# Products of a conditioning vector with its weights, taken four units of weights at a time

## The chip, the core and the metric

The kernel runs on one core of a Trainium2 chip. The metric is the device time of one execution in microseconds (us); the time of a version is the median of its runs. In the profile PE is TensorE's products, PEld its loads of weights, DVE VectorE, ACT ScalarE, POOL GpSimd, SP the queue of SyncE, which here issues most transfers.

## The reference

Two blocks follow each other. The first has two layers over 512 latent tokens and, in its first layer, 256 context tokens, all of 1024 features, in fp32:

```python
def mixer_layer(x, cx, c, c_ctx, w_in, w_out, w_ada, b_ada, ...):
    shift, scale, gate = jnp.split(jax.nn.silu(c) @ w_ada + b_ada, 3, axis=-1)
    shift_c, scale_c, gate_c = jnp.split(jax.nn.silu(c_ctx) @ w_ada + b_ada, 3, axis=-1)
    h = x * (1.0 + scale[:, None]) + shift[:, None]
    hc = cx * (1.0 + scale_c) + shift_c
    (a_q, a_i, a_ff, a_fb, b_q, ...) = jnp.split(h @ w_in, SPLIT_AT, axis=-1)
    ...
    y = jnp.concatenate([y_a, y_b, y_c, y_d], axis=-1) * jax.nn.silu(g_lat)
    x_new = layer_norm(alpha * x + gate[:, None] * (y @ w_out), ln_g, ln_b)
```

The two conditioning vectors c and c_ctx have 1024 numbers each; w_ada has 1024 rows and 3072 columns in each layer. Mixer A (y_a) is a gated recurrence, B, C and D are attention of three kinds. Shift and scale of a layer are wanted before its h, the gate at the layer's end. The second block (a gated mixture of four branches and an MLP) doesn't use w_ada.

## The kernel before

**Products.** The large products (of h with w_in, for instance) are made from a high and a low part of either factor, in three products (`mm3`): each unit of weights, 128 x 1024 numbers, is loaded by SP's queue as `raw` and split into `whi` and `wlo` on whichever of ScalarE, VectorE and GpSimd is free. The products with w_ada are fp32 throughout and take `raw` as it is, 4,096 bytes in each partition. The stationary factor is `cs`, 128 rows by 32 columns, of which two hold silu(c) and silu(c_ctx) for one k (128 of the 1024 rows of w_ada). Four k's stand side by side in the array: k goes to column group q = k % 4 and to the PSUM rows 32q to 32q + 31, and k + 4 is added to the same rows. One fp32 product is two instructions in the profile. A chunk of 512 columns is 8 products (16 instructions) from 4 units with 2 k's each; a chunk of 256 columns is 8 products from 2 units with 4 k's each. A chunk's bank is then copied to SBUF by ScalarE (`row`), and a product with a matrix that selects adds the four groups (`co_mod` for shift and scale, the rest of `g_ada_gate` for the gate).

**Chunks.** Layer 0's shift and scale are made at the start in eight chunks of 256 columns. Layer 1's shift and scale are a filler named mod in layer 0: four chunks of 512 columns. Each layer's gate is a filler named gate: two chunks of 512 columns. So there are eight chunks of 512 columns.

**The order of the work.** The program is emitted by a planner that keeps estimates of when engines and data will be ready. Work in flight (attention in the order c, b, d of its mixers, with a few units at a time; the two pairs of mixer A; evacuations) is a list of generators that yield what they wait for. In each turn the first of them that is ready goes on; only when none is ready does the current filler go on (`turn`). Fillers are the products with w_in and w_ada. `choose` takes up the next one:

```python
early = f.name[1:2].isdigit() and any(x.name[:1] in "bd" for x in self.todo[:i])
if early and self.early >= self.cfg["early"][self.l] and not self.forced:
    continue
if f.need == 0 or self.M.live * Mem.G + f.need <= self.cfg["cap"] or self.forced:
```

`M.live * Mem.G` is the planner's account of SBUF in bytes of a partition, `cap` is 200,000. The written order of layer 0 behind c and v is `b fq0 d g4 g2 mod fq1 g0 gate g6 g5 g3 g7 g1`, that of layer 1 `b fq0 fq1 g4 g5 gate d mod g0 g2 g3 g1 g6 g7` (mod is left out there). b and d make keys, queries and values of two attention mixers (their needs are 28,000), fq0 and fq1 the q and the forget gates of mixer A's two pairs (25,000), g0 to g7 gate columns (12,000). `early` bars the g's while b or d is still to be taken. A pair of mixer A begins when its fq is through and the pair before it has ended; attention of d begins when b's units are through and d's keys are prepared.

The loader (`wfill`, called by `wnext` for each unit and by some fillers in between) keeps up to 2 units ready and 2 more loading. When one unit is ready it makes no second one if the account and 8,192 would pass `capw`, 194,000; a further raw unit wants 4,096 below it. When the current filler has no more units to load it calls `choose` for the next, and when no filler is left every turn does.

**The account in layer 0.** The unchanged program's own account reads, in bytes: 179,328 when mod is taken (behind fq0, past d and the g's); at the loader's next call 176,320 with one unit of mod, so 172,224 without; 186,048 when mod's first chunk begins; between 162,304 and 178,816 without the units of w_ada while the six chunks are emitted; 178,816 when gate is taken, 174,656 when fq1 is, 144,448 when d is. In layer 1 it reads 149,824 when gate is taken and 164,672 when d is, in gate's second chunk.

After the planner, the tile framework orders each engine's instructions once more; two neighbours in the code may be parted there. SBUF addresses follow from the recorded lifetimes of all pieces, and a piece that takes the place of an earlier one waits for its last reader.

Of the kernel before, what the change touches and what calls it, by code (L numbers as in the profile page):

```python
# [24 lines left out]
# column starts in w_in of the first block  # L25
# [5 lines left out]
# units of packed w_in  # L31
U_F, U_Q, U_G, U_C0, U_C1, U_C2, U_C3 = 0, 4, 6, 14, 18, 22, 26

# columns of the per-partition vectors
# [16 lines left out]
# broadcast rows  # L51
# [37 lines left out]
def pack(inp):  # L89
# [67 lines left out]
    # constants of the shapes  # L157
# [14 lines left out]
    # second block  # L172
# [32 lines left out]
class Quiet:  # L205
    """Stands for an engine while lifetimes are recorded."""
# [5 lines left out]
class Est:  # L212
    """Estimates, while instructions are emitted, of when engines and data will be ready: the order of emission follows."""
# [7 lines left out]
    def touch(self, ap):  # L221
        """The times of a tensor and the granules of it (128 elements) that ap covers."""
        key = (ap.tensor.name, ap.offset, ap.ap)
        hit = self.memo.get(key)
        if hit is None:
            row = ap.ap[0][0]
            at = np.zeros(1, np.int64)
            if len(ap.ap) > 1 and row > 128:
                at[0] = ap.offset % row
                for s, n in ap.ap[1:]:  # L230
                    if s and n > 1:
                        k = np.append(np.arange(0, n, max(1, 128 // abs(s))), n - 1)
                        at = np.unique((at[:, None] + s * k).ravel())
            at = np.unique(at // 128)
            hit = self.memo[key] = (key[0], at, int(at[-1]) + 1)
        name, at, need = hit
        for d in (self.w, self.r):
            if name not in d:
                d[name] = np.zeros(max(need, 48))
            elif len(d[name]) < need:  # L240
                d[name] = np.append(d[name], np.zeros(need - len(d[name])))
        return self.w[name], self.r[name], at
# [24 lines left out]
class Eng:  # L267
    """An engine whose instructions are timed as they are emitted."""
# [29 lines left out]
class Filler:  # L298
    """A stretch of the tensor engine's main work: its units of weights, and the memory it wants. A gate is taken up only
    after all before it."""  # L300
# [5 lines left out]
class Act:  # L306
    """Work in flight: a generator that yields what it waits for."""
# [6 lines left out]
class Tl:  # L314
    """A piece of SBUF with its own tensor."""
# [14 lines left out]
class Mem:  # L330
    """SBUF by lifetimes. A first emission (plan None) only records them; place() then gives each piece its address."""
# [29 lines left out]
    def place(self):  # L361
        """Addresses for the recorded lifetimes. After its last use a piece rests for as long as there is room elsewhere;
        the long-lived and then the larger pieces choose first."""
        n = len(self.log)
        size = np.array([r[0] for r in self.log])
        f0 = np.array([n + 1 if r[1] is None else r[1] for r in self.log])
        ends = [[] for _ in range(n + 2)]
        for i in range(n):
            ends[f0[i]].append(i)
        for share in np.arange(1.0, 0.5, -0.02):  # L370
            rest = f0.copy()
            resting, use = [], 0
            for t in range(n):
                resting += ends[t]
                use += size[t]
                while use > share * self.n and resting:
                    i = resting.pop(0)
                    rest[i] = t
                    use -= size[i]
            for i in resting:  # L380
                rest[i] = n + 1
            for long in (300, 100, 200, 500, 50):
                at = self.fit(size, f0, rest, long)
                if at is not None:
                    self.share = share, long
                    return at
        raise MemoryError(f"peak {self.peak * self.G} of {self.n * self.G}")
# [26 lines left out]
class Pb:  # L414
    """Banks of PSUM."""
# [9 lines left out]
class Psum:  # L425
# [3 lines left out]
    def pick(self, n, est):  # L429
        """The free banks that have been read first, and when."""  # L430
# [28 lines left out]
class K:  # L459
# [18 lines left out]
    # ---- short forms  # L478
# [3 lines left out]
    def best(self, n, **costs):  # L482
        """The engine that would be through first; costs in ns for each of n columns."""
# [43 lines left out]
    def scale(self, out, a, s):  # L527
        """out = a times a column s."""
# [21 lines left out]
    # ---- time  # L550
# [43 lines left out]
    # ---- work in flight  # L594
# [11 lines left out]
    def after(self, *keys):  # L606
        """Until no work of these keys is in flight."""
# [8 lines left out]
    def room(self, n):  # L616
        """Until n bytes more would fit; given up when nothing else can go on."""
# [60 lines left out]
    def choose(self):  # L678
        """Takes up the first filler for which there is room."""
# [20 lines left out]
    def filled(self, *names):  # L700
        """Until these fillers are through."""
        return self.until(lambda: all(n in self.ndone for n in names))

    def units(self, us, f, window):
        """f(u) for every u, up to so many at a time."""
# [11 lines left out]
    # ---- weights  # L717
# [28 lines left out]
    def more(self):  # L746
        """Weights of a further filler."""
# [17 lines left out]
    def g_fm(self, parts, evac):  # L765
        """parts: [(hi, lo, n)]; evac(i, bank) for each."""
# [15 lines left out]
    def g_tm(self, tiles, evac, pre=True, ku=2, rounds=None, hook=None):  # L782
        """tiles: [(t, hi(k) ap, lo(k) ap, columns)]; a unit of weights has ku k's; rounds: which units are gone through at
        a time."""
# [33 lines left out]
    # ---------------------------------------------------------------- setup  # L818
# [25 lines left out]
    def load_late(self):  # L844
        """Constants that are wanted later."""
# [22 lines left out]
    # ---------------------------------------------------------------- ada  # L868
# [11 lines left out]
    def g_ada_chunk(self, res, n=512):  # L880
        """The product with n columns, the k's in four parts of the rows."""
        yield (self.bank(),)
        ps = self.new_bank()
        for u in range(n // 128):
            raw, = self.wnext()
            yield (raw,)
            for kk in range(1024 // n):
                k = u * (1024 // n) + kk
                q = k % 4
                self.nc.tensor.matmul(ps[32 * q:32 * q + 32, :n], self.cs[:, k, :], raw[:, kk * n:(kk + 1) * n],  # L890
                                      start=k < 4, stop=k >= 4, tile_position=(0, 32 * q))
            self.M.free(raw)
# [20 lines left out]
    def g_ada_mod(self, l, js):  # L913
        """shift and 1 + scale, feature-major: mod[:, kind * 8 + k, (lat, ctx)]."""
# [57 lines left out]
    # ---------------------------------------------------------------- a layer  # L972
# [8 lines left out]
    def htiles(self, ncol):  # L981
        """ncol(t): columns for token tile t, 0 to leave it out."""
# [7 lines left out]
    def consts_layer(self, l):  # L990
# [14 lines left out]
        if l == 1:  # L1005
# [9 lines left out]
            # f = lb + (1 - lb) (1 + tanh) / 2  # L1015
# [5 lines left out]
    # fillers  # L1021
# [9 lines left out]
    def rope_tm(self, out, src, t, G, d, isq=False, e2="*"):  # L1031
        """out = rotated src, both [128, G, d]; queries come out times d^-0.5."""
# [12 lines left out]
    def g_c(self):  # L1045
        """Rotated k and q of mixer C, token-major."""
# [19 lines left out]
    def g_bd(self, which):  # L1066
        """k, q and v of mixers B and D: raw for B, rotated for D."""
# [33 lines left out]
    def g_fq(self, pair):  # L1101
        """2 silu(q) of two heads and their forget gates."""
# [24 lines left out]
    def g_g(self, m):  # L1127
        """2 silu of the gate columns of y[m]."""
# [9 lines left out]
    def yput(self, m, t):  # L1138
        """One of the two factors of 2 y[m]; the second one closes it."""
# [19 lines left out]
    # attention  # L1159
    def stack4(self, stage, dst, eng="*", n=4):  # L1160
        """Transposes n x [128, 128] of stage into dst [128, n, 128]."""
# [6 lines left out]
    def kstack(self, src, tag):  # L1168
        """src(t) gives a staged [128, 512] for each key tile."""
# [10 lines left out]
    def stage_c(self, raw, p, t, isq):  # L1180
        """[128, 4, 32]: keys hi hi lo lo, queries hi lo hi lo."""
# [9 lines left out]
    def stage_k64(self, src):  # L1191
        """[128, 2, 64] keys: hi hi, lo lo for either head."""
# [5 lines left out]
    def stage_q64(self, src):  # L1198
        """[128, G, 64] queries: hi lo for each head."""
# [6 lines left out]
    def trans_p(self, p, n):  # L1206
        """[128 q, n keys] over itself as [128 keys, n // 128, 128 q]."""
# [10 lines left out]
    class Seg:  # L1218
        """A part of the attention: prep() makes the keys, unit(u) does one of us."""
# [3 lines left out]
    def pvs(self, st, nqt):  # L1223
        """The banks of outputs of st, made when first wanted."""
# [79 lines left out]
    def headnorm(self, pv, gcol, m, eps):  # L1304
        """y[m] gets rms of each 64-feature half of the banks pv, times gcol."""
# [30 lines left out]
    def co_prep_b(self, t):  # L1336
        """rms norms and rotations of mixer B's k and q."""
# [121 lines left out]
    # mixer A  # L1459
# [15 lines left out]
    def co_head(self, pair, hh, qs, f, res):  # L1475
        """The products within the chunks, the state before each chunk and the decayed q of a head, both directions."""
# [13 lines left out]
        for i in range(7):  # L1490
# [13 lines left out]
            # forward rows: q of the upper halves, k of the lower ones; backward rows mirrored  # L1504
# [60 lines left out]
    # ---------------------------------------------------------------- epilogue of a layer  # L1565
    def co_transpose_h(self, xh, hh, o, mulv, addv):
        """h = xh^T * mulv + addv as high and low parts at columns o.. of hh."""
# [15 lines left out]
    def epilogue(self, l, xsrc, xdst):  # L1583
        """The rest of a layer: leaves the next h (or xn for the second block)."""
# [130 lines left out]
    def co_rms(self, x, t, g, hl):  # L1715
        """xn = rms(x) * g, transposed, into the columns of token tile t of hl."""
# [11 lines left out]
    # ---------------------------------------------------------------- second block  # L1728
# [7 lines left out]
    def co_gelu(self, dst, h, n):  # L1736
        """dst = gelu(2 h), the tanh form; h is freed."""
# [13 lines left out]
    def co_lnorm(self, dst, src, after=None):  # L1751
        """dst = (src - mean) / std over the free axis of 256."""
# [15 lines left out]
    # gmlp  # L1768
# [52 lines left out]
    # convolutions  # L1821
# [114 lines left out]
    # nsa  # L1936
# [186 lines left out]
    def g_nsa_in(self):  # L2123
        """The token-major projections."""
# [52 lines left out]
    # gates and the sum of the branches  # L2177
# [8 lines left out]
    def proj(self, n, m, hi, lo, t):  # L2186
        """acc[m] += (t + 1) * projection of branch n."""
# [172 lines left out]
    # ---------------------------------------------------------------- the whole  # L2360
# [49 lines left out]
    def layer_fill(self, l, xsrc, xdst):  # L2410
# [13 lines left out]
        for name in self.cfg["order"][l].split():  # L2424
# [5 lines left out]
            elif name == "gate":  # L2430
                g, u, need = lambda: self.g_ada_gate(l), self.w_ada(l, (4, 5)), 12000
            elif name == "mod":
                if l == 1:
                    continue
                g, u, need = lambda: self.g_ada_mod(1, (2, 0, 3, 1)), self.w_ada(1, (2, 0, 3, 1)), 12000
# [80 lines left out]
```

## Time and profile before

| | |
|---|---|
| median of 3 runs | 2021.99 us |
| lowest, highest | 2017.59, 2022.09 us |
| span of the profiled execution | 2020.4 us |
| own time of the profiled execution | not listed apart from its span; the median is 1.6 us above the span |
| TensorE busy | 1892.4 us, 94% of the span |
| mean granted clock of TensorE | 0.979 |

Nearly all instructions are issued through one line of a helper (L283), so groups are told apart by the tiles that they write and read: `raw,cs` are the products with w_ada, `h,whi`, `whi,h` and the like those with w_in, `qm,kh` products of mixer A, `p` and `kc,qs` attention. A group's busy time counts overlapping instructions once.

### The profile page before, as it was taken

Reading aid. Unit: us, or ns where it says so; the run is one execution under the profiler, and the core shown is the slowest. Engines: PE = TensorE matmul, PEld = TensorE weight load, DVE = VectorE, ACT = ScalarE, POOL = GpSimd, SP = SyncE. Lnnn points to the kernel's source line nnn. Section 1 sums busy time; section 2 is a strip of 40 time slices with the busy share of each in tenths; the row PEclk is TensorE's granted clock in tenths of the full one; section 3 lists DMA queues with packets and bytes.
Section 4 is the critical chain, followed back from the end, with each engine's and each line's share of the span. In section 5 each row is a group of like instructions: output and inputs, shape, how many; then the busy total and the mean of one; then the engine's idle time right before and its main releaser. Section 6 shows DMA issues by size and latency. Waiting matters only on the chain.

```text
span 2020.4 us, 28590 instructions
## 1 busy us (share of the span) xinstructions
PE 1892.4 (94%) x11270; PEld 1571.6 (78%) x11270; DVE 1295.5 (64%) x2202; ACT 621.0 (31%) x1274; POOL 636.4 (31%) x583
## 2 busy tenths in 40 slices
PE   6899889889999999979899989899999999999999
PEld 4688657789877788867787777877878787888887
DVE  2558885686557738787967878874533566545542
ACT  2245434414540135544335231143432211100100
POOL 1314662374232414565633353421121220000000
PEclk9999999999999999999999998999999999999999
DMA  8112241001132401103124221111232222233122
GB/s 348 53 32 71 72 142 47 17 17 57 32 115 84 157 1 43 38 21 106 43 63 141 98 101 66 67 58 48 81 128 87 99 73 84 83 115 115 53 84 73
DMA packets 46807, 162.32 MB, mean 80 GB/s; under 512 B 5312, under 2 KB 5824, under 8 KB 46416
## 3 DMA queue, kind: packets, MB, share of 16 engines
q1 hardware_dynamic: 43648, 151.63, 21.9%
q10 hardware_dynamic: 3024, 8.85, 1.3%
q8 instruction: 89, 1.46, 0.3%
q14 instruction: 46, 0.38, 0.1%
HBM read 152.58 MB, written 5.26 MB: 78 GB/s over the span
## 4 chain that ended last, share of the span: by engine, by line
PE 41%; DVE 11%; POOL 3%; issue 2%; ACT 2%; DMA 0%; ACTq 0%; DVEq 0%; POOLq 0%
PE banks L283 41%; DVE cacc L283 2%; POOL t L283 1%; DVE sm L283 1%; DVE wlo L283 1%; DVE kh L283 1%; DVE t L283 1%; ACT p L283 1%; DVE att L283 1%; DVE p L283 1%; DVE h L283 1%; DVE whi L283 0%; POOL h L283 0%; DMA ld<-gws 0%; DVE gt L283 0%
## 5 line engine op out<-in xcount | busy, mean ns | idle before, releaser
L283 PE MATMUL banks<-h,whi 128*128 128x512 f32 (+1 forms) x1968 | 583.9, 380 | 4.4 <-ACT h L283 2.1
L283 PEld LDWEIGHTS banks<-h,whi 128*128 128x128 f32 x1968 | 353.6, 191 | 66.5 <-POOL h L283 2.5
L283 PE MATMUL banks<-h,wlo 128*128 128x512 f32 (+1 forms) x984 | 369.4, 376 | 0.3 <-DVE wlo L283 0.3
L283 PE MATMUL banks<-whi,h 128*128 128x256 f32 (+3 forms) x1344 | 336.1, 333 | 17.2 <-DVE h L283 7.9
L283 DVE TENSOR_TENSOR wlo<-raw,whi 128x1024 fp32r<-128x1024 f32 (+1 forms) x174 | 216.6, 1248 | 94.9 <-PE banks L283 59.5
L283 PEld LDWEIGHTS banks<-whi,h 128*128 128x128 f32 x1344 | 235.5, 193 | 41.9 <-DVE h L283 9.8
L283 POOL TENSOR_TENSOR wlo<-raw,whi 128x1024 fp32r<-128x1024 f32 (+2 forms) x42 | 103.4, 2464 | 482.8 <-PE banks L283 314.6
L283 PE MATMUL banks<-wlo,h 128*128 128x256 f32 (+3 forms) x672 | 220.2, 328 | 7.4 <-POOL wlo L283 3.7
L283 PEld LDWEIGHTS banks<-h,wlo 128*128 128x128 f32 x984 | 187.6, 191 | 35.8 <-DVE wlo L283 1.0
L283 ACT ACTIVATE p<-banks,sm 128x768 f32<-128x768 f32 (+5 forms) x192 | 141.3, 739 | 107.5 <-DVE sm L283 90.6
L283 DVE TENSOR_REDUCE sm<-banks 128x1 f32<-128x768 f32 (+5 forms) x192 | 139.9, 750 | 49.1 <-PE banks L283 41.4
L283 PE MATMUL banks<-whi,hid 128*128 128x512 f32 x512 | 159.5, 392 | 0.0
L283 DVE CAST whi<-raw 128x1024 fp32r<-128x1024 f32 (+2 forms) x105 | 79.3, 759 | 112.8 <-DMA raw<-wm 66.0
L283 PEld LDWEIGHTS banks<-wlo,h 128*128 128x128 f32 x672 | 129.7, 193 | 19.0 <-DVE wlo L283 5.0
L283 ACT CAST whi<-raw 128x1024 fp32r<-128x1024 f32 (+2 forms) x83 | 82.8, 1002 | 193.3 <-PE banks L283 98.1
L283 PEld LDWEIGHTS banks<-whi,hid 128*128 128x128 f32 x512 | 96.1, 188 | 21.5
L283 PE MATMUL banks<-ident,p 128*128 128x128 f32 x656 | 97.1, 278 | 15.7 <-ACT p L283 5.7
L283 ACT COPY p<-banks 128x768 f32<-128x768 f32 (+5 forms) x122 | 75.6, 626 | 106.5 <-PE banks L283 96.8
L283 PE MATMUL banks<-qm,kh 128*128 128x128 f32 x640 | 91.9, 294 | 17.3 <-DVE att L283 8.1
L283 PEld LDWEIGHTS banks<-qm,kh 128*128 128x128 f32 x640 | 83.1, 204 | 29.4 <-issue 9.8
L283 PEld LDWEIGHTS banks<-ident,p 128*128 128x128 f32 x656 | 74.5, 141 | 34.3 <-ACT p L283 8.7
L283 POOL TENSOR_TENSOR t<-t,mhalf 128x1 f32<-128x1 f32 (+5 forms) x51 | 64.4, 1266 | 115.9 <-DVE t L283 112.3
(331 smaller groups left out, 3220.8 us busy)
## 6 DMA issues: line engine op xcount, KB each, us to landing
raw<-wm SPq DMA_DIRECT2D x64, 512.0 KB, 3.7
raw<-win SPq DMA_DIRECT2D x60, 512.0 KB, 3.6
raw<-wada SPq DMA_DIRECT2D x48, 512.0 KB, 4.8
raw<-wgate SPq DMA_DIRECT2D x32, 512.0 KB, 3.2
raw<-wout SPq DMA_DIRECT2D x24, 512.0 KB, 3.5
raw<-w2f SPq DMA_DIRECT2D x10, 512.0 KB, 3.2
xr<-xtok SPq DMA_DIRECT2D x6, 512.0 KB
x<-z SPq DMA_DIRECT2D x6, 512.0 KB, 2.6
```

The source lines that it names most:

```text
L283: return f(*a, **kw)
```

## The change

`g_ada_chunk` takes the units of a chunk of 512 columns in one go (four calls of `wnext`), waits until all four have landed, issues the eight products (sixteen instructions) behind each other and frees the four units at the end. Before, it took one unit, waited for it, issued its two products and freed it, four times, and other work could come between. Chunks of 256 columns keep their two steps of one unit each. The memory that the fillers gate and mod ask for before they are taken goes from 12,000 to 24,000 bytes. Comments and docstrings are removed as well, with the numbers of the lines kept.

```diff
     def g_ada_chunk(self, res, n=512):
...
         yield (self.bank(),)
         ps = self.new_bank()
-        for u in range(n // 128):
-            raw, = self.wnext()
-            yield (raw,)
-            for kk in range(1024 // n):
-                k = u * (1024 // n) + kk
-                q = k % 4
+        per = 1024 // n
+        for us in ((0,), (1,)) if n == 256 else (range(4),):
+            raws = [self.wnext()[0] for _ in us]
+            yield (*raws,)
+            for k in range(us[0] * per, us[-1] * per + per):
+                q, raw, kk = k % 4, raws[k // per - us[0]], k % per
                 self.nc.tensor.matmul(ps[32 * q:32 * q + 32, :n], self.cs[:, k, :], raw[:, kk * n:(kk + 1) * n],
                                       start=k < 4, stop=k >= 4, tile_position=(0, 32 * q))
-            self.M.free(raw)
+            self.M.free(*raws)
...
             elif name == "gate":
-                g, u, need = lambda: self.g_ada_gate(l), self.w_ada(l, (4, 5)), 12000
+                g, u, need = lambda: self.g_ada_gate(l), self.w_ada(l, (4, 5)), 24000
...
-                g, u, need = lambda: self.g_ada_mod(1, (2, 0, 3, 1)), self.w_ada(1, (2, 0, 3, 1)), 12000
+                g, u, need = lambda: self.g_ada_mod(1, (2, 0, 3, 1)), self.w_ada(1, (2, 0, 3, 1)), 24000
```

## Rows read from the trace of the kernel before

**Rows 1.** The page, its head and its part on busy time.

```profile
span 2020.4 us, 28590 instructions
PE 1892.4 (94%) x11270; PEld 1571.6 (78%) x11270; DVE 1295.5 (64%) x2202; ACT 621.0 (31%) x1274; POOL 636.4 (31%) x583
```

**Rows 2.** Groups by form: count, busy us, mean ns, idle us before and its releasers.

```profile
L283 PE MATMUL banks<-raw,cs 128*32 128x512 f32 x128 | 29.9, 604 | 0.1
L283 PE MATMUL banks<-raw,cs 128*32 128x256 f32 x128 | 13.2, 463 | 9.7 <-DVE t L283 8.4 <-DMA raw<-wada 1.3
```

**Rows 3.** Stretches, the instructions on cs alone; columns as in rows 4.

```profile
215.65:312.00 96.35, 22.77 (x96) 3.38 (x96) 0.00 (x0) 0.98 0.34 111
936.15:960.60 24.45, 7.10 (x32) 1.11 (x32) 0.00 (x0) 1.00 0.45 151
```

**Rows 4.** Stretches, all instructions, with the head of the columns.

```profile
core 0: us, PE busy (x) PEld busy (x) DVE busy (x) ACT busy (x) POOL busy (x), PEclk, DMA share, GB/s
225.00:325.00 100.00, 87.20 (x618) 60.19 (x615) 80.10 (x134) 38.40 (x82) 66.30 (x61) 0.98 0.34 111
375.00:450.00 75.00, 62.22 (x497) 58.11 (x496) 61.34 (x84) 20.32 (x42) 49.38 (x46) 0.89 0.03 8
936.15:960.60 24.45, 24.45 (x183) 15.95 (x182) 20.40 (x31) 10.28 (x19) 16.18 (x16) 1.00 0.45 151
```

**Rows 5.** Stretches, the instructions that read or write h alone.

```profile
216.00:309.00 93.00, 0.00 (x0) 0.00 (x0) 0.00 (x0) 0.00 (x0) 0.00 (x0) 0.98 0.34 114
375.00:450.00 75.00, 21.89 (x146) 19.29 (x146) 0.00 (x0) 0.00 (x0) 0.00 (x0) 0.89 0.03 8
475.00:600.00 125.00, 80.22 (x426) 63.49 (x426) 0.00 (x0) 0.00 (x0) 0.00 (x0) 1.00 0.21 68
```

**Rows 6.** Groups by form of TensorE from 215 to 312 us.

```profile
L283 PE MATMUL banks<-qm,kh 128*128 128x128 f32 x192 | 27.3, 290 | 2.9 <-DVE sm L283 1.8 <-DVE att L283 1.1
...
L283 PE MATMUL banks<-kc,qs 128*128 128x512 f32 x10 | 4.8, 498 | 4.9 <-ACT p L283 4.0 <-DVE att L283 1.0
```

**Rows 7.** Timeline of TensorE: start us, us, operation, count; bursts and what follows.

```profile
215.65 1.91 PE L283 MATMUL banks<-raw,cs 128*32 128x512 f32 x12
...
257.95 1.05 PE L283 MATMUL banks<-raw,cs 128*32 128x512 f32 x2
258.93 0.61 PE L283 MATMUL banks<-kc,qs 128*128 128x512 f32 x2
...
272.66 1.05 PE L283 MATMUL banks<-raw,cs 128*32 128x512 f32 x4
273.64 0.38 PE L283 MATMUL banks<-kc,qs 128*128 128x256 f32 x1
273.95 1.07 PE L283 MATMUL banks<-raw,cs 128*32 128x512 f32 x8
274.95 1.60 PE L283 MATMUL banks<-qm,kh 128*128 128x128 f32 x12
...
955.07 1.91 PE L283 MATMUL banks<-raw,cs 128*32 128x512 f32 x12
956.91 1.66 PE L283 MATMUL banks<-kb,qs 128*128 128x512 f32 x8
...
959.62 1.05 PE L283 MATMUL banks<-raw,cs 128*32 128x512 f32 x4
```

**Rows 8.** Timeline of weight loads, a burst's and the next; TensorE's next product.

```profile
288.02 0.14 PEld L283 LDWEIGHTS banks<-raw,cs 128*32 128x32 f32 x4 [0.16 <-issue]
289.01 0.19 PEld L283 LDWEIGHTS banks<-p,vc 128*64 128x64 f32 x2 [0.84 <-issue]
...
289.01 0.43 PE L283 MATMUL banks<-p,vc 128*64 128x128 f32 x2
```

**Rows 9.** The units of w_ada: time to landing; issues on SP's queue.

```profile
DMA to landing us min/median/max: 3.4/4.8/10.4
...
217.60 65.96 SPq L283 DMA_DIRECT2D raw<-wada  x17
```

## The prediction

> **What bounds the kernel now.** I read the page first. TensorE is busy 94% of the span, no other engine over 64% [rows 1]: whatever frees TensorE time frees time of the kernel, unless the freed time lies where TensorE already waits. So the question is where the changed products stand. The groups by form give the products of 512 columns as 128 instructions with 29.9 us of busy time, less than half of 128 times their mean of 604 ns, so they overlap; those of 256 columns are a group of their own, which the diff leaves as it is [rows 2]. Of the 29.9 us, 22.8 lie in 215.65 to 312 us (six chunks: four of mod, two of layer 0's gate) and 7.1 in 936 to 961 us (layer 1's gate) [rows 3].
>
> Then the stretches. Where the six chunks run, TensorE is busy 87.2 of 100 us, VectorE 80.1 and GpSimd 66.3; later in layer 0, at 375 to 450 us, it is busy 62.2 of 75 and the granted clock averages 0.89. Layer 1's two chunks stand in a stretch without any idle TensorE [rows 4]. What the engine has to do besides matters as much: from 216 to 309 us not one product reads h, while 375 to 450 us has 21.9 us of them and 475 to 600 us 80.2 [rows 5]. In the first stretch the ada chunks are thus the only filler between attention and the halving levels of mixer A, whose decays and masks run on VectorE and GpSimd (the products kh by qm alone take 27.3 us of TensorE) [rows 6].
>
> **The change: the runs.** The timeline of TensorE shows what a chunk costs. A burst of two or four instructions takes its place for 0.98 us, from its start to the start of the next other product (272.66 to 273.64). One of eight takes 1.00 (273.95 to 274.95): two units reach all four column groups, and the second comes almost free. One of twelve takes 1.84 (955.07 to 956.91) [rows 7]. A run of sixteen fills the same four steps of the column groups as twelve (8 + 8 against 8 + 4), so I price it at 1.84 too.
>
> From 215.65 to 959.62 us I count 26 bursts, of which the first and the last are shown [rows 7]. Layer 0 has 18 short and 2 long ones: 18 x 0.98 + 2 x 1.84 = 21.3 us. Layer 1 has 5 short and 1 long: 4.9 + 1.84 = 6.7 us. In all 28.0 us. Eight whole runs would take 8 x 1.84 = 14.7 us, so 13.3 us is the most that TensorE gains.
>
> Not every run will be whole. The burst at 257.95 has only two instructions: the first k of a unit went out, then two products of attention, then the rest, though the code yields only between units [rows 7]. I count five bursts of two in layer 0 and none in layer 1. If half of layer 0's six chunks break once, they take 6 x 1.84 + 3 x 0.98 = 14.0 us and save 7.3; layer 1 saves 6.7 - 3.7 = 3.0.
>
> In layer 1 all 3.0 us count, the engine being full there. In layer 0, 12.8 of 100 us are idle, and each small burst may have stood in a gap that now stays empty; I let 87% count, 7.3 x 0.87 = 6.4 us. The bounds are 0 (every burst sat in a gap that nothing else fills) and 13.3.
>
> What follows a burst speaks for the short figure: the weight load behind one waits 0.84 us, but the next product starts 0.98 us after the burst did, so the wait lies inside the burst [rows 8]. The Trainium skill (TensorEngine Tiling (Array Packing), Key Properties) says that a change of tiling mode drains TensorE. Were that drain a cost beside the burst, each of some fifteen bursts saved would give 0.84 us more, 12.6 us in all, and the time would be near 2000 us; the two rows just cited do not bear it out, for load and product start together when the burst ends.
>
> **The wait for four units.** A chunk now starts when its fourth unit has landed, 4.8 us after issue in the median and at most 10.4 [rows 9]. The loader may not run ahead in layer 0: when the first chunk begins, the account stands at 186,048 bytes, and another unit made ready asks for 8,192 below a limit of 194,000; the fourth unit is issued when the chunk asks for it. Queued behind the waiting chunk are only later fillers, since attention and mixer A are emitted in front of fillers; they keep TensorE 87% busy there [rows 4], so I cost the wait at nothing. Without that cover it is 6 x 4.8 = 28.8 us. Behind a unit on SP's queue stand the next units, the bias rows of gate and w_in's units for fq1; a unit issued later delays those, and the 17 issues from 217.60 us on are spread over 66 us already [rows 9]. Evacuation (one ScalarE copy and two to eight small products per chunk) is unchanged in number. A run of 1.84 holds up what is queued behind it 0.86 us longer than a burst of 0.98, eight times, 6.9 us at most; the fewer bursts give that back, and I cost it at nothing.
>
> **The doubled need.** This can move whole fillers. When mod is taken the account reads 179,328; with 24,000 it no longer fits under 200,000. At the loader's next call it reads 172,224 without mod's unit: d (28,000) misses by 224 bytes, the g's are barred until d is taken, mod fits with 196,224. So mod stays first and its first unit is asked for a little later. After mod the matter is open. Gate was taken at 178,816 and no longer fits there. Without ada's units the account then moves between 162,000 and 179,000, and from 172,000 down d comes first, before fq1 and gate. I expect d in gate's place: its products of h, now behind fq1's, go into the stretch that has none, gate and fq1 go behind it, and mixer A's second pair starts later. In layer 1 gate (149,824) and d (164,672, or four kilobytes more with the unit still held) still fit, and the order stays.
>
> What that move is worth, the trace can't show; two stretches bound it. The first has 12.8 us of idle TensorE that d could fill. The second shows d's products beside a pair of mixer A: 12.8 us idle in 75, and at a mean clock of 0.89 some 22% of it, 16.5 us, at half speed, which is 8.2 us of work [rows 4, 5]. So from 12.8 gained to 21.0 lost. I take 0, as attention's last part no longer waits for d but VectorE and GpSimd, busy already, get d's splits and evacuations.
>
> **The sum.** 3.0 + 6.4 = 9.4 us off a span of 2020.4 gives 2011.0; the median of the three runs lies 1.6 us above that span, so 2012.6 us.
>
> **The rivals.**
> - Nothing to measure: the small bursts were gap fillers. With mixer A on VectorE and GpSimd setting the pace from 216 to 309 us, TensorE waits where it worked, and only layer 1's 3.0 us is left: 2019 us, within the bound. For it: ScalarE's and VectorE's p and sm end TensorE's idle time there [rows 6]. Against: d, gate and fq1 stand ready to fill it.
> - Slower: d beside mixer A's first pair repeats the stretch of 375 to 450 us, idle and at the lower clock, with nothing given back later: 2012.6 + 21.0 = 2033.6 us. It is slower than before by more than the measurement's bound from 15.5 us added. For it: TensorE idles 0.17 of that stretch, 0.13 of the first. Against: the lack of d's keys no longer stands in attention's way later. The Trainium skill (Perfetto Trace Analysis, Optimization Strategy) reads repeated gaps on the busiest engine as a sign that the next tile finds no SBUF; four held units of 4,096 bytes in a full account would make more of them, which would end on this side. No row here shows a gap laid to memory.
> - Faster than forecast: d fills the idle 12.8 us and brings no new idle: 2012.6 - 12.8 = 1999.8 us.
> - The change doesn't do what it says: runs broken at every second k. Then bursts of four stay and it is the first rival's time.
>
> **How the numbers follow.** A difference under 0.3% (6.1 us: 2015.9 to 2028.1) can't be told from none. Forecast 0.40 (its own range 2006 to 2017), nothing to measure 0.28 (broken runs among it), slower 0.20, faster than forecast 0.12. Faster: 0.12, nine tenths of the forecast and a little of the next case, 0.52. Same: 0.29. Slower: 0.19. The range reaches from 1999 to 2033, to the centres of the outer cases, which leaves out half of each, 0.16.
>
> **What would show it.** Right: the products of 512 columns at 14 to 19 us of busy time instead of 29.9, in eight to eleven runs; layer 1's stretch some 3 us shorter; products of h before 309 us; layer 0's end earlier by about 6 us. Wrong, if the group's busy time stays above 25 us; if the idle time of 225 to 325 us grows by what the group loses; if gate follows mod as before; or if mixer A's second pair ends so late that the last products of layer 0 wait for it.

## The result, and the profile after

The changed kernel takes 2033.22 us (median of 4 runs, 2030.14 to 2035.37), the kernel before 2022.04 beside it (2017.59 to 2024.91): 11.2 us more, a ratio of 1.0054 with the interval [1.0037, 1.0071]. It is slower by more than the 0.3% that the prediction set as its bound. The profiled execution has a span of 2033.6 us at a mean granted clock of 0.974 (0.979 before), so the time is accounted for against 2020.4 us. Two of the kernels below had one execution in a slower state of the chip (c2 with 2609.51 us, e1 with 3403.58); their times here are medians without it, while the expectations that quote 2036.99 us for c2 count it in.

The page's head and busy time, of after:

```profile
span 2033.6 us, 28564 instructions
PE 1889.9 (93%) x11270; PEld 1578.5 (78%) x11270; DVE 1302.7 (64%) x2201; ACT 631.5 (31%) x1278; POOL 617.3 (30%) x580
```

TensorE's busy time fell by 2.5 us, its idle time rose from 128.0 to 143.7 us. So work was saved, and more than that was lost in waiting. The group of the changed products, by form (busy us, mean ns | idle us before and its releaser), and below it stretches of after, the instructions on cs alone:

```profile
L283 PE MATMUL banks<-raw,cs 128*32 128x512 f32 x128 | 23.7, 608 | 1.5 <-DMA raw<-wada 1.5
```

The stretches:

```profile
core 0: us, PE busy (x) PEld busy (x) DVE busy (x), PEclk, DMA share, GB/s
212.00:262.00 50.00, 13.97 (x64) 2.22 (x64) 0.00 (x0) 0.97 0.42 141
489.00:526.00 37.00, 4.89 (x32) 0.96 (x32) 0.00 (x0) 0.86 0.22 72
944.00:965.00 21.00, 4.89 (x32) 0.95 (x32) 0.00 (x0) 1.00 0.40 143
```

Against [rows 2, 3] the busy time went from 29.9 to 23.7 us. Mod's four chunks stand where they stood; layer 0's gate, which followed mod before 312 us, now stands at 489 to 526 us. The timeline of TensorE (start us, us, operation, count) shows the runs:

```profile
246.22 1.92 PE L283 MATMUL banks<-raw,cs 128*32 128x512 f32 x14
248.06 0.62 PE L283 MATMUL banks<-kc,qs 128*128 128x512 f32 x2
...
250.78 1.05 PE L283 MATMUL banks<-raw,cs 128*32 128x512 f32 x2
251.76 1.60 PE L283 MATMUL banks<-qm,kh 128*128 128x128 f32 x12
253.29 1.07 PE L283 MATMUL banks<-raw,cs 128*32 128x512 f32 x8
...
523.59 1.92 PE L283 MATMUL banks<-raw,cs 128*32 128x512 f32 x16
525.44 0.82 PE L283 MATMUL banks<-qm,kh 128*128 128x128 f32 x5
```

A whole run holds its place for 1.85 us (523.59 to 525.44), as priced. There are 16 bursts in place of 26, 13 of them in layer 0; only two of the eight chunks went out whole.

Now the stretches of after, all instructions; the first two answer to [rows 4]:

```profile
core 0: us, PE busy (x) PEld busy (x) DVE busy (x) ACT busy (x) POOL busy (x), PEclk, DMA share, GB/s
225.00:325.00 100.00, 82.45 (x632) 65.70 (x630) 79.54 (x133) 35.47 (x77) 58.69 (x55) 0.93 0.21 72
375.00:450.00 75.00, 72.16 (x548) 62.45 (x547) 46.23 (x99) 36.39 (x83) 16.20 (x18) 0.98 0.12 38
450.00:625.00 175.00, 158.88 (x1070) 132.04 (x1070) 124.39 (x228) 63.09 (x140) 75.71 (x70) 0.96 0.23 76
500.00:550.00 50.00, 42.92 (x299) 35.38 (x299) 40.53 (x78) 19.03 (x46) 25.10 (x28) 0.90 0.24 78
```

The last part of layer 0 in the kernel before, same columns:

```profile
450.00:625.00 175.00, 169.99 (x1230) 148.22 (x1229) 105.84 (x243) 71.94 (x172) 60.18 (x54) 1.00 0.21 71
```

The poor stretch at 375 to 450 us is gone (idle 2.8 us instead of 12.8). The end of the layer has it instead: 16.1 us idle where 5.0 were, at a clock of 0.96 instead of 1.00. One nearly pays for the other: from the start to the end of layer 0 (defined below) TensorE is idle 58.1 us before and 63.5 after, 5.4 more. These two stretches, before and then after:

```profile
0.00:616.40 616.40, 558.30 (x3935) 456.88 (x3935) 403.68 (x760) 245.25 (x535) 245.14 (x227) 0.98 0.24 83
```

```profile
0.00:620.00 620.00, 556.47 (x3939) 457.80 (x3939) 410.65 (x768) 249.81 (x536) 231.51 (x218) 0.97 0.24 83
```

What moved is mixer A's second pair, of which this is the row of the products qm by kh between 340 and 650 us (ns least, median and most; first and last start). Before:

```profile
L283 PE MATMUL banks<-qm,kh x192: 270/275/579, 389.4 to 463.4; 128*128 128x128 f32 x192
```

After:

```profile
L283 PE MATMUL banks<-qm,kh x192: 272/275/436, 471.6 to 551.5; 128*128 128x128 f32 x192
```

It starts 82.2 us later, since its filler fq1 now comes behind d and two g's, and so gate and the pair share the layer's last stretch. TensorE's waits there, in after (releaser: us in all, times, longest):

```profile
PE banks L283 <- ACT p L283: 4.1, 3, 1.9
PE banks L283 <- DVE qs L283: 2.7, 1, 2.7
PE banks L283 <- ACT yh L283: 1.8, 1, 1.8
PE banks L283 <- ACT f L283: 1.5, 2, 1.2
```

These are its four largest waits: it waits for the work of VectorE and ScalarE on attention and on the pair; the same stretch of before has 1.1 us of waits on p and 0.7 on qs.

For the accounts below I cut the span in three: to the first product of ident by z, which opens layer 0's last step (616.4 us before, 620.0 after); to the last product of wlo by yh, which ends layer 1's output (1151.7 and 1172.0); and the rest. By that cut after loses 3.6 us in layer 0 and 16.7 in layer 1, and gains 7.1 in the rest: 13.2, the difference of the spans. Read alone, this puts the blame on layer 1. A stretch of 25 us there, all instructions, columns as above, in after:

```profile
950.00:975.00 25.00, 15.11 (x84) 9.65 (x82) 18.87 (x18) 8.28 (x15) 23.85 (x24) 0.91 0.27 100
```

and in the experiment e4, which differs from after by layer 1's chunks alone:

```profile
950.00:975.00 25.00, 21.14 (x129) 15.38 (x128) 22.57 (x32) 9.16 (x16) 17.94 (x17) 0.86 0.17 56
```

In after GpSimd is busy 23.85 of 25 us and TensorE waits for it, as its timeline shows behind the second run:

```profile
962.11 1.16 PE L283 MATMUL banks<-qm,kh 128*128 128x128 f32 x8 [3.26 <-POOL qm L283]
967.11 2.03 PE L283 MATMUL banks<-qm,kh 128*128 128x128 f32 x8 [2.86 <-POOL kh L283]
```

Whether the runs bring that about, or chance in how the planner shares the work out, is what the experiments had to tell.

### The profile page after: what moved, and what is told of

Same layout as the page of the kernel before. It is cut to its first block, busy times and chain, and to the rows that moved or that the text cites. A ratio compares the mean times of both kernels' runs of the same rounds, so it can differ in the third digit from the quotient of the medians.

```text
span 2033.6 us, 28564 instructions
## 1 busy us (share of the span) xinstructions
PE 1889.9 (93%) x11270; PEld 1578.5 (78%) x11270; DVE 1302.7 (64%) x2201; ACT 631.5 (31%) x1278; POOL 617.3 (30%) x580
## 5 line engine op out<-in xcount | busy, mean ns | idle before, releaser
L283 DVE TENSOR_TENSOR wlo<-raw,whi 128x1024 fp32r<-128x1024 f32 (+1 forms) x174 | 227.2, 1311 | 98.4 <-PE banks L283 47.0
L283 ACT CAST whi<-raw 128x1024 fp32r<-128x1024 f32 (+1 forms) x89 | 89.0, 1005 | 235.9 <-PE banks L283 179.4
L283 PEld LDWEIGHTS banks<-ident,p 128*128 128x128 f32 x656 | 78.2, 147 | 35.4 <-ACT p L283 11.2
L283 PE MATMUL banks<-wlo,hid 128*128 128x512 f32 x256 | 99.9, 390 | 0.0
```

What stands on the lines that cost most here:

```text
L283: return f(*a, **kw)
```

## The experiments

All times stand against the kernel before, run beside them on the same chip. The theories at the start were "order" (the doubled need puts d ahead of fq1 and gate, and that costs), "runs" (the run of sixteen itself costs in layer 1, where it stands beside mixer A), "calls" (four calls of the loader in a row upset the loads there), and later "chance" or "deal": any small shift lets the planner choose another order of emission and another share of the work for VectorE and GpSimd, and so moves the time.

**The need alone, e1_need_only.** The kernel before with both needs raised, its chunks unit by unit as they were:

```diff
-... self.w_ada(l, (4, 5)), 12000
+... self.w_ada(l, (4, 5)), 24000
-... self.w_ada(1, (2, 0, 3, 1)), 12000
+... self.w_ada(1, (2, 0, 3, 1)), 24000
```

> Only the needs of mod and gate are doubled; chunks stay as before, unit by unit. The planner then takes d ahead of gate and fq1 in layer 0, as in the changed kernel. Theory 'order' (d's move costs the time, the runs save some 6 us): 2033 to 2042 us. Theory 'runs' (the wait for four held units and the long runs cost it): 2022 us, within 3. Theory 'chance' (any change of the emission moves work between VectorE and GpSimd and pieces in SBUF, and with it each layer by several us either way): anywhere from 2012 to 2034.

2040.88 us, ratio 1.0086 [1.0067, 1.0105], layer 0's end at 631.3 us. As "order" had it: with d (and g4 and g2 behind it) moved and the chunks as before, layer 0 is 14.9 us longer.

**The runs alone, e2_runs_only.** After, with both needs at 12,000:

> Only the runs of sixteen; the needs stay at 12,000. The planner takes gate right behind mod, as before the change, and d behind gate, ahead of fq1. Theory 'order', if gate's place is what counts: 2012 to 2018 us; if d ahead of fq1 is what counts, 2030 or more. Theory 'runs': 2033 us. Theory 'chance': anywhere from 2012 to 2034.

2039.79 us, ratio 1.0082 [1.0065, 1.0099]. It doesn't separate the two: the units that a chunk holds change the account, and the planner took d, g4 and g2 before fq1 here too, behind mod and gate. It does part gate's place from d's: gate follows mod as in the kernel before, and still layer 0 ends at 627.2 us and the last stretch, without any product on cs, has 19.6 us of idle time.

**Layer 1's runs alone, e3_runs_layer1_only.** Needs at 12,000, and

```diff
-        for us in ((0,), (1,)) if n == 256 else (range(4),):
+        for us in ((0,), (1,)) if n == 256 else (range(4),) if self.l else ((0,), (1,), (2,), (3,)):
```

> Runs of sixteen in layer 1's gate alone, needs of 12,000; layer 0 is the kernel before, and layer 1's fillers keep their order. Theory 'order': 2019 us (3 us less TensorE work, nothing else). Theory 'runs': 2030 to 2034, since between 742 and 1172 us the changed kernel fell behind by more in layer 1 than in layer 0. Theory 'chance': 2012 to 2034, and products that are far from the chunks in time are lengthened or shortened.

2029.24 us, ratio 1.0025 [1.0012, 1.0039]: slower, as "runs" said, though just below its range; "order" misses.

**Layer 0's part alone, e4_runs_layer0_only.** After, with layer 1's gate unit by unit:

```diff
-        for us in ((0,), (1,)) if n == 256 else (range(4),):
+        for us in ((0,), (1,)) if n == 256 else ((0,), (1,), (2,), (3,)) if self.l else (range(4),):
```

> The changed kernel with layer 1's gate made unit by unit again; layer 0 is that of the changed kernel. Theory 'order': 2034 to 2037 us, 3 us of TensorE work more than changed. Theory 'runs': 2022 to 2027, layer 1's loss gone. Theory 'chance': 2012 to 2034.

2019.72 us, ratio 0.9992 [0.998, 1.0004]: far below "order", a little below "runs". So far the runs of layer 1 seem to cost all of it.

**The loader's calls, e6_calls_spread and e7_calls_in_row.** After; in layer 1 e6 waits behind each of the four calls and then issues the run, e7 calls four times in a row and issues the products unit by unit.

```diff
-            raws = [self.wnext()[0] for _ in us]
+            raws = []
+            for _ in us:
+                raws.append(self.wnext()[0])
+                if self.l and n == 512:
+                    yield (raws[-1],)
             yield (*raws,)
```

```diff
-            yield (*raws,)
+            if not self.l or n == 256:
+                yield (*raws,)
...
+                if self.l and n == 512 and k % 2 == 0:
+                    yield (raws[k // 2],)
```

> The changed kernel; in layer 1's gate the four units are still held and the sixteen products go in one row, but the loader is called for one unit at a time, each time with a wait for that unit before the next call. Theory 'calls' (four calls of the loader in a row bring d's splits onto VectorE ahead of mixer A's steps, which is where 957 to 963 us showed them): 2018 to 2025 us, as with layer 1 unit by unit. Theory 'runs' (a long run or a late fourth unit stalls layer 1): 2031 to 2036 us, as changed. Theory 'chance' (any shift of the emission in layer 1 does this): either, and no rule.

> The changed kernel; in layer 1's gate the loader is called four times in a row and the units are held, but their products go unit by unit with a wait ahead of each, so other work can come between. Theory 'calls': 2031 to 2036 us. Theory 'runs': 2018 to 2025 us. Theory 'chance': either.

e6: 2035.89 us, 1.0066 [1.0047, 1.0086]; e7: 2027.41, 1.0033 [1.0018, 1.0048]. Without calls in a row it stays slow, with them it is the better one: the opposite of what "calls" says.

**Runs in layer 0 in the old order, e8_runs_old_order.** e4 with needs at 12,000 and the written order set to the one that the kernel before took:

```diff
-           order=("b fq0 d g4 g2 mod fq1 g0 gate g6 g5 g3 g7 g1",
+           order=("b fq0 mod gate fq1 d g4 g2 g0 g6 g5 g3 g7 g1",
```

> Runs of sixteen in layer 0, layer 1 unit by unit, needs of 12,000, and layer 0's written order set to the one in which the kernel before takes its fillers: b fq0 mod gate fq1 d and the g's. Theory 'order' (the runs save 6 to 10 us in layer 0 where the order is kept): 2011 to 2016 us, with layer 0 ended near 608 us instead of 616.4. Theory 'runs' (holding four units costs layer 0 too): 2022 or more. Theory 'chance': 2012 to 2034.

2031.46 us, ratio 1.0051 [1.0031, 1.0071], where "order" had 2011 to 2016; layer 0 ends at 615.4 us, 1.0 earlier than before, and layer 1, not touched, is 9.2 us longer. That is as large as the effects looked for.

**The control, c2_lag.** The kernel before with nothing changed but a constant of the planner's estimates. It alters no product and, here, not the order of the fillers, only what is emitted first in places and which engine takes a piece of work.

```diff
-    LAG = 90.0
+    LAG = 88.0
```

> The kernel before with one constant of the planner's estimates, the lag between engines, at 88 instead of 90 ns: the same fillers in the same order, chunks unit by unit, needs of 12,000, and only small shifts in the emission. Theories 'order', 'runs' and 'calls': 2022 us, within 3, as nothing of theirs is changed. Theory 'chance': off by 5 us or more either way.

2035.93 us, ratio 1.0066 [1.0045, 1.0087]: 15.0 us lost with the chunks as they were; in the profiled execution layer 1 is 14.2 us longer. At one LAG no stage table can therefore say what a part of the change costs. The rest repeats the comparison at other values.

**Before and after at other LAGs: p1_before_lag87, p2_after_lag87, p3_after_lag88, p4_before_lag91.** The edit is the constant.

> The kernel before with the planner's constant LAG at 87 instead of 90; the fillers come in the same order in both layers and the chunks are as before. Theory 'chance' (the order of emission and the share of the work between VectorE and GpSimd are dealt anew by any small shift, and the deal of the kernel before is a good one): slower than before, 2026 to 2040 us, the loss spread over layer 0 and layer 1. Theory 'runs' (the whole runs and the fillers' new order cost by themselves): within 4 us of before, 2017 to 2025.

> The kernel after with LAG at 87; its fillers keep the order of after. Theory 'chance': no telling where it ends, but within 7 us of the kernel before at LAG 87, on either side, so that the mean of the differences at LAG 87, 88 and 90 is near 0. Theory 'runs': 8 to 16 us above the kernel before at the same LAG.

> The kernel after with LAG at 88, beside the kernel before at LAG 88, which took 2036.99 us. Theory 'chance': 2020 to 2040 us, so not slower than that by more than 4. Theory 'runs': as much over the kernel before at this LAG as at 90, 2045 to 2053 us.

> The kernel before with LAG at 91: layer 0 as in the kernel before, in layer 1 the filler g4 comes before fq1. Theory 'chance': 2026 to 2040 us, layer 0's end within 2 us of 616.4 and layer 1 longer than 535.3 us. Theory 'runs': within 4 us of before.

2037.23, 2049.29, 2047.63 and 2026.77 us (ratios 1.0082 [1.0065, 1.0098], 1.0131 [1.0112, 1.015], 1.0119 [1.0098, 1.0141], 1.0022 [1.0009, 1.0034]). Both theories are half right: the constant moves the kernel before by up to 15.2 us, and the change costs 12.1 us at 87 and 10.6 at 88 as it costs 11.2 at 90.

**The halves at other LAGs.** f1 and f3 are e4 at 87 and 88, f2 and f4 are e3.

> LAG 87, layer 0 as in after (doubled need, whole runs), layer 1's gate unit by unit. At this LAG before took 2037.23 us, after 2049.29. Theory 'layer 1' (the run of sixteen in layer 1 is what costs, layer 0 gives about nothing): 2035 to 2040. Theory 'layer 0' (d ahead of gate and fq1 is what costs, the run in layer 1 is neutral): 2046 to 2052. Theory 'deal' (both stages move by some ten us with any change, and the sum of 11 to 12 us at three LAGs is a mean of many): anywhere between 2030 and 2055, with no agreement with LAG 90 (where it took 2019.72, 2.0 below before).

> LAG 87, layer 0 as in before, layer 1's gate in whole runs. Theory 'layer 1': 2046 to 2052, 10 or more above before's 2037.23. Theory 'layer 0': 2034 to 2040. Theory 'deal': anywhere between 2030 and 2055; at LAG 90 it was 8.3 us above before.

> LAG 88, layer 0 as in after, layer 1's gate unit by unit. At this LAG before took 2036.99 us, after 2047.63, with layer 0's end 17.7 us later and layer 1 as long as before. Theory 'layer 1': 2034 to 2040. Theory 'layer 0': 2045 to 2050, since the stage table puts the loss there. Theory 'deal': no agreement with LAG 87 and 90 on which part costs.

> LAG 88, layer 0 as in before, layer 1's gate in whole runs. Theory 'layer 1': 2045 to 2050. Theory 'layer 0': 2034 to 2040. Theory 'deal': no agreement with LAG 87 and 90 on which part costs.

2051.97, 2040.43, 2055.83 and 2027.57 us (1.0142 [1.0125, 1.016], 1.0086 [1.0071, 1.0102], 1.0162 [1.0145, 1.018], 1.0033 [1.0018, 1.0047]). The blame is turned round: at these LAGs layer 0's part costs, layer 1's runs cost little or nothing. That is the direction that "layer 0" gave; of its ranges only f1's is kept, f2 lies 0.4 us above, f3 5.8 above and f4 6.4 below.

**The old order at other LAGs.** g1 and g2 are e8 at 87 and 88.

> LAG 87; layer 0 with whole runs, need 12,000 and the fillers in the order of before (mod, gate, fq1, d); layer 1 unit by unit. At this LAG before took 2037.23 us with layer 0's end at 625.7, the layer 0 half of the change 2051.97 with 626.1, the whole change 2049.29 with 631.1. Theory 'order' (d ahead of gate and fq1 is what costs, whole runs cost nothing): layer 0's end 619 to 626, time 2030 to 2040. Theory 'runs' (whole runs cost in layer 0, in either order): layer 0's end 628 to 634, time 2044 to 2054. Theory 'deal': no agreement of this run with the one at LAG 88.

> LAG 88, else as the run at LAG 87. At this LAG before took 2036.99 us with layer 0's end at 615.9, the layer 0 half of the change 2055.83 with 634.8, the whole change 2047.63 with 633.6. Theory 'order': layer 0's end 609 to 617, time 2028 to 2040. Theory 'runs': layer 0's end 628 to 636, time 2046 to 2058. Theory 'deal': no agreement of this run with the one at LAG 87.

2025.22 and 2024.35 us (1.0019 [1.0004, 1.0033], 1.0017 [1.0004, 1.003]); layer 0 ends at 615.4 and 609.1 us. Both are below the ranges of "order" (by 4.8 and 3.7 us) and far below "runs". At these LAGs the runs without the new order gain 12.0 and 12.7 us.

The differences in time, each against the kernel before at the same LAG (us; each median less that of before beside it, then less what the LAG alone does, 15.2 us at 87 and 15.0 at 88):

| | LAG 90 | LAG 87 | LAG 88 | mean |
|---|---|---|---|---|
| whole change | +11.2 | +12.1 | +10.6 | +11.3 |
| layer 0's part (order and runs) | -2.0 | +14.2 | +18.3 | +10.2 |
| layer 1's runs | +7.5 | +2.7 | -10.0 | +0.1 |
| layer 0's runs, old order | +10.5 | -12.0 | -12.7 | -4.7 |

The intervals above reach 2 to 4 us to either side of a median, so by estimate a difference is told to some 5 us. Only the first row agrees from LAG to LAG; the means of the others are of numbers that differ by 17 to 23 us.

And what the traces say of the order (us; the second pair's first product, TensorE's idle time from 450 to 625 us, layer 0's end, layer 1's length):

| fillers of layer 0 | LAG | pair from | idle | layer 0 | layer 1 |
|---|---|---|---|---|---|
| fq1 before d: before | 90 | 389.4 | 5.0 | 616.4 | 535.3 |
| c2 | 88 | 389.3 | 5.0 | 615.9 | 549.5 |
| p1 | 87 | 395.5 | 8.6 | 625.7 | 551.0 |
| p4 | 91 | 389.8 | 5.9 | 617.9 | 536.6 |
| e3, f2, f4 | 90, 87, 88 | 390.6, 396.7, 386.3 | 5.0, 8.5, 6.1 | 617.8, 627.3, 612.7 | 541.3, 554.8, 543.4 |
| e8, g1, g2 | 90, 87, 88 | 392.6, 397.8, 393.8 | 8.7, 7.4, 8.4 | 615.4, 615.4, 609.1 | 544.5, 551.6, 557.7 |
| d, g4, g2 before fq1: after, p2, p3 | 90, 87, 88 | 471.6, 480.9, 476.2 | 16.1, 19.7, 25.5 | 620.0, 631.1, 633.6 | 552.0, 555.2, 548.7 |
| e4, f1, f3 | 90, 87, 88 | 472.4, 476.7, 476.7 | 16.1, 19.3, 23.0 | 620.7, 626.1, 634.8 | 537.3, 559.9, 553.0 |
| e1, e6, e7 | 90 | 485.6, 473.8, 475.2 | 18.7, 18.1, 16.8 | 631.3, 622.4, 622.3 | 544.0, 551.9, 539.8 |
| e2 | 90 | 499.3 | 19.6 | 627.2 | 547.4 |

The third and fourth columns don't overlap: with fq1 behind d the pair starts at 471.6 us or later and the idle time is 16.1 us or more, without that at 397.8 or earlier and 8.7 or less. The same holds of TensorE's idle time from the start to layer 0's end: 56.8 to 60.9 us in the ten kernels with fq1 first, 63.5 to 77.0 in the ten with d first. Layer 0's end itself overlaps, with means of 617 and 627 us; every length here is of one execution, and kernels whose layer 0 is the same differ by up to 5.0 us there (p2 and f1). The last stretch of layer 0 at LAG 88, all instructions, columns as above, of p3 (the most idle time):

```profile
450.00:625.00 175.00, 149.53 (x1048) 124.75 (x1047) 118.90 (x210) 59.95 (x140) 84.87 (x80) 0.95 0.24 76
```

and of g2:

```profile
450.00:625.00 175.00, 166.62 (x1175) 143.31 (x1175) 115.84 (x250) 74.12 (x171) 53.05 (x50) 1.00 0.22 75
```

VectorE and GpSimd have 203.8 us of work in p3's stretch (118.90 + 84.87), 168.9 in g2's; I take the rest for the pair's share, which comes late. The last column, layer 1, spreads by 25 us among kernels whose layer 1 is unit by unit (535.3 to 559.9), and before has the best of it.

## Why the prediction was wrong

By the three parts of the span, the forecast of 2011.0 us missed the 2033.6 by 22.6: layer 0 was to end 6.4 us earlier and ended 3.6 later (10.0 of the miss), layer 1 was to be 3.0 shorter and was 16.7 longer (19.7), and the rest, which was to stay, came out 7.1 shorter. So two steps failed: the 0 for the doubled need, which is a loss in layer 0, and the 3.0 us of layer 1 that were to count in full, in a layer that a shift of the emission alone made 1.3 to 15.7 us longer (p4, c2, p1). The sum had no term for such a shift. The runs bear out a cause for the loss in layer 0; that of the larger one in layer 1 stays open.

**The doubled need: the place was right, the value 0 was not.** The place: d did come in gate's place, gate and fq1 went behind it, and mixer A's second pair started later, all as forecast. The value was taken at 0 between 12.8 us gained and 21.0 lost. Layer 0's part less the same runs in the old order gives the order's price: -12.5 at LAG 90 (-2.0 - 10.5), +26.2 at 87, +30.9 at 88, a mean of +14.9, which numbers so far apart leave uncertain; e1 gives +19.2 of time and +14.9 in layer 0. By layer 0's end alone it is +5.3, +10.7 and +25.7 at 90, 87 and 88 (e4 less e8, f1 less g1, f3 less g2), a mean of 13.9, and TensorE's idle time up to there is 5.8, 13.5 and 17.1 us more. All are losses, the one at LAG 90 hardly beyond what one execution tells. I had looked at where d would go, not at where the pair would stop: I read its old stretch (12.8 us idle at a clock of 0.89) as a price that d might bring forward, while the price moved back with the pair, to the end of the layer, where (this is not shown) little is left to fill it. The old stretch wasn't the pair's price alone, though: with runs in the old order and the pair at its old place it is idle for 4.3, 3.2 and 3.6 us (e8, g1, g2), and 225 to 325 us for 17.3, 19.0 and 19.9 instead of 12.8. Only the sum over the layer tells what the order costs. The sentence that named this, the last products of layer 0 waiting for the pair, stood only among the signs of a wrong forecast.

The Trainium skill (Perfetto Trace Analysis, Optimization Strategy) says that one and the same gap recurring on the engine that should be full may mean that the next tile finds no memory. No listed wait of TensorE in the last stretch is laid to memory: all end on another engine's result (the largest, 4.1 us, on ScalarE's p); memory acts a step earlier, in the account that put d before fq1.

**Layer 1's 3.0 us "all count": not shown.** The full engine there was the reason given. But the run replaces time that is dealt anew: against the same layer 0, layer 1 with runs is 14.7 us longer, 4.7 shorter and 4.3 shorter (after, p2, p3 less e4, f1, f3), and 6.0, 3.8 and -6.1 us longer with the old layer 0 (e3, f2, f4 less before, p1, c2). A term of 3 us can't be seen in that. At LAG 90 it is a loss both times (6.0 and 14.7), and after's 16.7 us in layer 1 is most of what separates it from before; that is the place, but the runs were not shown to cause it.

**The bursts.** Price right: 1.85 us a run against 1.84 forecast. Count too good: 16 bursts, not 8 to 11; five of layer 0's six chunks broke, not half. The group lost 6.2 us, at 23.7 outside the 14 to 19 forecast. Of layer 0's 6.4 us the runs in the old order seem to give 6.0 at its end (-1.0, -10.3 and -6.8 against before, p1 and c2). I don't take that as confirmed: e8 has 13 bursts in layer 0 and gains least, g1 and g2 have 16 and gain most (counted as rows of the timeline).

**The wait for four units at nothing: right.** 1.5 us of TensorE's idle time ends on these units in after. Whether the later issues delayed other work was not shown.

**Products of h before 309 us: right** (9.66 us of them from 216 to 309 us, none before [rows 5]), and still not a gain: TensorE's idle time from 225 to 325 us rose from 12.8 to 17.6 us. That is one of the signs named for a wrong forecast: layer 0's changed products lost 3.9 us of busy time (22.77 to 13.97 + 4.89), and the idle time there grew by as much or more. In that stretch the first rival, bursts as gap fillers, is nearer to the measurement than the forecast.

**The range.** It reached to 2033 for a cause that could give 21 us. What it had no term for is the deal: 4.7 to 15.2 us at three LAGs with the chunks unchanged, all losses, which suggests that the kernel before stands at a good deal. The rival "slower" gave 2033.6 us and the kernel took 2033.22, with d's move as the cause. That the time fits is luck: what the runs show of d's move lies in layer 0, which lost 3.6 us, and there beside the second pair rather than the first; most of the loss is layer 1's, which the rival didn't name.

What stays open: what made layer 1 16.7 us longer at LAG 90; why the order is no loss in time at LAG 90 (e4 against e8), where layer 0's end still shows 5.3 us; which piece of layer 1's work, handed to another engine, costs most; and whether the runs have a small effect of their own. No version was clearly faster than before; e4 is level with it.

## What to carry to other kernels

When an edit changes what a planner counts, follow the moved work to the end of its stage: ask which chain now starts later (here 82 us) and whether anything is left to fill its waits there. Before explaining a difference of half a per cent in a kernel whose order a program decides, run the unchanged kernel with a harmless shift; if that alone moves the time by as much, a cause needs the same sign at several shifts, or a trace mark that separates all kernels. Take the mark over a whole stage: a stretch with more idle time may only have taken over that of another.

## What was not expected of the hardware

The same run of sixteen took 1.92 us at a granted clock near 1 and 3.64 us in e8's layer 0, where TensorE had just idled 3.36 us, waiting for VectorE's att: the granted clock was 1.00 at 280 to 281 us, in that gap, and 0.50 during the run, the lower of the two levels (1.2 against 2.4 GHz), and the run is 1.9 times as long. The run and the product ahead of it in e8's timeline:

```profile
282.41 0.58 PE L283 MATMUL banks<-kc,qs 128*128 128x256 f32 x1 [3.36 <-DVE att L283]
282.93 3.64 PE L283 MATMUL banks<-raw,cs 128*32 128x512 f32 x16
```

and two stretches, all instructions, columns as above, the first in the gap and the second in the run:

```profile
280.00:281.00 1.00, 0.00 (x0) 0.00 (x0) 1.00 (x1) 0.00 (x0) 0.63 (x1) 1.00 0.47 188
283.00:286.00 3.00, 3.00 (x16) 0.52 (x16) 2.94 (x6) 1.34 (x4) 1.23 (x2) 0.50 0.00 0
```

Runs at that place took 3.64 us in g1 and g2 as well, behind gaps of 2.62 and 2.64 us. A run issued whole can thus stand whole in such a slow moment.
